# Where the tiles of a decoder trunk's matmuls lie in SBUF: tile widths rounded up to 64 bytes, and pads between pools

## The chip, the cores and the metric

The kernel runs on one core of a Trainium2 chip. The metric is the device time of one execution in microseconds; lower is better. The engines are called as in the profile: PE is TensorE's matmul and PEld its weight load, DVE is VectorE, ACT is ScalarE, POOL is GpSimd and SP is SyncE. A PE matmul has two operands in SBUF: the stationary one (the weights, 128 columns, loaded by a weight load of its own before the matmul) and the moving one (256 or 512 columns, streamed through the array).

## What is computed

A trunk of two decoder layers on 512 tokens of width 1024, in float32. The first layer mixes tokens by a gated delta rule, the second by windowed attention with sinks; both also attend to 256 fixed memory tokens, and both end in a SwiGLU feed-forward of width 2816.

```python
def swiglu(h, w_gate_up, w_down):
    gu = h @ w_gate_up
    return (jax.nn.silu(gu[..., :D_FF]) * gu[..., D_FF:]) @ w_down

for layer in range(DEPTH):                        # 2
    h = rms_norm(x, ln_mix[layer])
    mkv = mem_n @ w_mem_kv[layer]
    if layer < N_A_LAYERS:
        mix_out, mem_q = gated_deltanet_mixer(h, gdn_w_in[a], ...)
    else:
        proj = h @ swa_w_q[bl]
        mix_out = sliding_window_attention(q, shared_k, shared_v, swa_sinks[bl])
    mem_o = memory_attention(mem_q, mem_k, mem_v)
    x = x + jnp.concatenate([mix_out, mem_o], axis=-1) @ w_out[layer]
    x = x + swiglu(rms_norm(x, ln_ffn[layer]), w_gate_up[layer], w_down[layer])
    ...
return rms_norm(x, ln_final)
```

## The kernel before

**Matmuls in three parts.** Every large product keeps float32 accuracy by splitting each operand into a high and a low part (`split`, L166: a rounding copy on ACT writes the high part, a subtraction on DVE the low part). `mm3` (L191) then issues three matmuls for one tile of 128 x 128 weights: high weights by high activations, high weights by low activations, low weights by high activations. They run in the format float32r, four bytes an element. 2,436 of them have 512 moving columns and 3,672 have 256; together they are most of what PE does.

**Where the operands live.** SBUF is given out by pools that lie one behind the other in each partition. From the left: `const` (constants, gains, small vectors), `w` (raw weights and a ring of three pairs of split weights, `whi` and `wlo`), `acta` and `actb` (eight pairs of split activations each, `h` and `l`; layer 0 and layer 1 use the two in turn for the input of the feed-forward and for its first eight activations), `x` (the residual stream). From the right, one after the other in time: `early` and `gdn` of the first layer, `ffn0`, `swa`, `ffn1`. A feed-forward pool holds, among others, the split sums of tokens (`T`, the tiles of `token_sums`, eight), the activations beyond the eighth (`ac8` to `ac11`), and work tiles (`fg`, `fu`, `fs`, `ws`).

**The feed-forward.** For a pair of columns `quarters` makes seven products of 256 columns from eight quarter blocks in place of eight, out of sums of weights (`wraw`, `ws`) and sums of tokens (`T`); three of the seven use `h` tiles directly, four use `T`. Each product is four `mm3`, so 12 matmuls in a row. The first four gate columns are plain products of 512 columns. The way down (`wdn`) is again made of `mm3` with 512 columns over the activations `h`, then `ac8`, `ac9` and so on.

**Order.** The program is written in the order of the source, and a scheduler places independent instructions on each engine's queue by priority and by which buffers are free. Within one engine the queue runs in order.

**Small tiles that the change touches.** `scores` (L710) makes three vectors of eight numbers (`mx`, `den`, `nm`) for each block of heads, and `weigh` (L748) a fourth, `es`. `token_sums` makes `minus` (four negated gains) once a layer and `fc` (128 x 256) four times a layer, in one buffer. `eps` holds two constants.

Of the kernel before, what the change touches and what calls it, by code (L numbers as in the profile page):

```python
# [9 lines left out]
F32 = mybir.dt.float32  # L10
# [5 lines left out]
PSUM = bass.MemoryType.PSUM  # L16
DRAM = bass.MemoryType.DRAM

P = 128
T = 512  # L20
D = 1024
KD = D // P
H = 6
NC = 4
# [2 lines left out]
DFF = 2816  # L27
FT = DFF // P
EPS = 1e-6
NEG = -1e30  # L30
BASE = 32
NB = P // BASE
# [34 lines left out]
def constants():  # L67
# [4 lines left out]
    c[:, C_ONE:C_ONE + P] = 1.0  # L72
    c[:, C_CAUS:C_CAUS + P] = np.where(i[None, :] >= i[:, None], 0.0, NEG)
    c[:, C_BAND:C_BAND + P] = np.where(i[None, :] > i[:, None], 0.0, NEG)
# [12 lines left out]
class Builder:  # L87
# [6 lines left out]
    def t(self, pool, shape, dtype=F32, tag=None, bufs=None, name=None):  # L94
        self.n += 1
        nm = f"{name or tag}_{self.n}"
        kw = {}
        if tag is not None:
            kw["tag"] = tag
        if bufs is not None:  # L100
            kw["bufs"] = bufs
        return pool.tile(shape, dtype, name=nm, **kw)

    @contextmanager
    def banks(self, **bufs):
# [121 lines left out]
    def build(self):  # L227
        tc, nc, a = self.tc, self.nc, self.a
        with ExitStack() as st:
            opened = lambda name, **kw: tc.tile_pool(name=name, bufs=1, reuse_waits="tile", **kw)  # L230
            pool = lambda name, **kw: st.enter_context(opened(name, **kw))
            cp = pool("const")
            self.wpool, self.apool = pool("w"), pool("acta")
            self.dpool = pool("scratch", space=DRAM)
            self.load_constants(cp)
            self.weng = nc.vector
            with opened("layer0", side="right") as self.mpool:
                with self.banks(pj=3, g=2, sc=3):
                    with opened("early", side="right") as ep:
                        self.mem_and_norm(ep)  # L240
                        self.gates(ep)
                    with opened("gdn", side="right") as gp:
                        mix = self.gdn(gp)
                    self.bpool, xp = pool("actb"), pool("x")
                    self.x = [self.t(xp, [P, T], F32, f"x{k}") for k in range(KD)]
                    for k in range(KD):
                        nc.sync.dma_start(self.x[k], a["xT"][:, k, :])
                    self.rstd, self.cosT, self.sinT = (self.t(xp, [P, T], F32, n) for n in ("rstd", "cosT", "sinT"))
                    h = self.output(xp, 0, mix, self.bpool)
            with opened("ffn0", side="right") as fp, self.banks(pj=2, g=6):  # L250
                self.ffn(fp, xp, 0, h, self.apool, rope=True)
            with self.banks(pj=2, g=1, qk=1, pt=2, sc=1):
                with opened("swa", side="right") as sp:
                    mix = self.swa(sp)
                h = self.output(xp, 1, mix, self.apool)
            with opened("ffn1", side="right") as fp, self.banks(pj=2, g=6):
                self.ffn(fp, xp, 1, h, self.bpool)

    def load_constants(self, cp):
        nc, a = self.nc, self.a  # L260
        c = self.t(cp, [P, C_N], F32, "consts")
        g = self.t(cp, [P, G_N], F32, "gains")
        s = self.t(cp, [P, 24], F32, "small")
        nc.sync.dma_start(g, a["gains"])
        self.consts, self.gains, self.small = c, g, s
        self.ident = c[:, C_ID:C_ID + P]
        self.U = c[:, C_U:C_U + P]
        self.ones = c[:, C_ONE:C_ONE + P]
        self.caus = c[:, C_CAUS:C_CAUS + P]
        self.band = c[:, C_BAND:C_BAND + 2 * P]  # L270
        self.one = c[:, C_ONE:C_ONE + 1]
        v = self.t(cp, [P, 2], F32, "eps")
        nc.vector.memset(v[:, 0:1], EPS)
        nc.vector.memset(v[:, 1:2], EPS * EPS * P)
        self.eps, self.epsq = v[:, 0:1], v[:, 1:2]
# [178 lines left out]
    def gdn(self, gp):  # L454
# [89 lines left out]
        for h0 in (0, 3):  # L544
# [3 lines left out]
            for h, t in zip(range(h0, h0 + 3), ts):  # L548
# [6 lines left out]
                sq = self.t(gp, [P, T], F32, "sq", 1)  # L555
                nc.scalar.activation(sq, t, AF.Square, scale=math.sqrt(EPS) * P)
                q2.append(self.t(self.dpool, [P, T], F32, f"q2{h}"))
# [152 lines left out]
    def scores(self, pool, q, kk, win):  # L710

        nc = self.nc
        own = "pt" in self.pbufs
        half = [slice(0, 64), slice(64, P)]
        sm = [self.t(pool, [P, 2, 2, 2 * P], F32, "sm", 4 if own else 2) for _ in range(2)]
        sm = [t[:, n] for t in sm for n in range(2)]
        mx = self.t(pool, [P, 2 * NC], F32, "mx", 2)
        den = self.t(pool, [P, 2 * NC], F32, "den", 2)
        nm = self.t(pool, [P, 2 * NC], F32, "nm", 2)
        for n0 in range(0, NC, 2):  # L720
            if own:
                two = self.bank("qk", [P, 2, 2, 2 * P])
                ps = [two[:, b] for b in range(2)]
            else:
                ps = [self.bank("sc" if n0 else "g", [P, 2, 2 * P]) for _ in range(2)]
            for n in (n0, n0 + 1):
                ks = slice((n - 1) * P if n else 0, (n + 1) * P) if win else slice(0, ML)
                c0 = P if win and n == 0 else 0
                for b in range(2):
                    self.scored = self.mm(ps[b][:, n - n0, c0:], q[half[b], n * P:(n + 1) * P], kk[half[b], ks])  # L730
            for b in range(2):
                i = b * NC + n0
                if win:
                    for n in (n0, n0 + 1):
                        c0 = 0 if n else P
                        nc.vector.tensor_tensor_reduce(  # L736
                            out=sm[n][:, b, c0:], in0=ps[b][:, n - n0, c0:], in1=self.band[:, c0:], scale=1.0,
                            scalar=NEG, op0=ALU.add, op1=ALU.max, accum_out=mx[:, b * NC + n:b * NC + n + 1])
                else:
                    nc.vector.tensor_reduce(out=mx[:, i:i + 2], in_=ps[b], op=ALU.max, axis=AX.X)  # L740
                    self.ts(nm[:, i:i + 2], mx[:, i:i + 2], -0.125, ALU.mult)
                    for n in (n0, n0 + 1):
                        i = b * NC + n
                        self.fn(sm[n][:, b, :], ps[b][:, n - n0, :], AF.Exp, scale=0.125, bias=nm[:, i:i + 1],
                                accum_out=den[:, i:i + 1])
        return sm, mx, den, nm

    def weigh(self, pool, scores, vv, m, out, sinks):  # L748

# [1 line left out]
        win = sinks is not None  # L751
        own = "pt" in self.pbufs
        half = [slice(0, 64), slice(64, P)]
        sm, mx, den, nm = scores
        if win:
            sk = sinks.unsqueeze(2).to_broadcast([P, 2, NC])
            v4 = lambda ap: ap.rearrange("p (b n) -> p b n", b=2)
            self.stt(v4(mx), v4(mx), 0.125, sk, ALU.mult, ALU.max)
            self.ts(nm, mx, -1.0, ALU.mult)
            es = self.t(pool, [P, 2 * NC], F32, "es", 2)  # L760
            self.tt(nc.vector, v4(es), v4(nm), sk, ALU.add)
            self.fn(es, es, AF.Exp)
            for n in range(NC):
                c0 = 0 if n else P
                for b in range(2):
                    i = b * NC + n
                    self.fn(sm[n][:, b, c0:], sm[n][:, b, c0:], AF.Exp, scale=0.125, bias=nm[:, i:i + 1],
                            accum_out=den[:, i:i + 1])
            self.tt(nc.vector, den, den, es, ALU.add)
# [3 lines left out]
        for n in range(NC):  # L773
# [3 lines left out]
            p = sm[n][:, :, k0 * P:]  # L777
# [21 lines left out]
            for n, t in pf.items():  # L799
                for j in range(1 if win and n == 0 else 0, 2):  # L800
                    for b in range(2):
                        v = vv[n - 1 + j][:, half[b]] if win else vv[j][:, m * P + 64 * b:m * P + 64 * b + 64]
# [23 lines left out]
    def ffn(self, fp, xp, layer, h, apool, rope=False):  # L826
# [3 lines left out]
        acts, sums, open_pairs, places = [], [], [], []  # L830
# [12 lines left out]

        def put(u):
            n = len(acts)
            acts.append(self.pair(apool) if n < KD else self.pair(fp, f"ac{n}"))
            self.split(u, *acts[-1])

        def ring():
# [30 lines left out]
        for f0, half in ((0, 12), (12, 10)):  # L880
# [16 lines left out]
            for m in range(tail):  # L897
                ps = self.bank("pj")
                for j in (0, 6):
                    n = min(6, half - j)  # L900
# [8 lines left out]
        if tail < KD:  # L909
# [9 lines left out]
            for t in parts:  # L919
                acc = self.acc[:, t]  # L920
                for m in range(tail, KD):
# [3 lines left out]
                    x = self.x[m][:, t]  # L925
# [11 lines left out]
    def token_sums(self, fp, layer, j, h):  # L937


        q = T // 2  # L940
        if j == 0:
            self.minus = self.t(fp, [P, 4], F32, "minus")
            self.ts(self.minus, self.gains[:, G_FFN[layer] + 4:G_FFN[layer] + 8], -1.0, ALU.mult)
        g0, g1 = (self.gain(G_FFN[layer], j + i) for i in (0, 4))
        n1 = self.minus[:, j:j + 1]
        x0, x1 = self.x[j], self.x[j + 4]
        c = self.t(fp, [P, q], F32, "fc")
        raw = [self.t(fp, [P, T], F32, "ws", 4) for _ in range(2)]
        t = [x[:, i * q:(i + 1) * q] for x in raw for i in range(2)]
        self.ts(c, x0[:, q:], g0, ALU.mult)  # L950
# [272 lines left out]
```

## Time and profile before

| | |
|---|---|
| median of 3 runs | 1167.77 us (1166.97 to 1170.53) |
| the profiled execution | 1172.62 us, of which the span from the first to the last instruction is 1170.9 us |
| granted TensorE clock | 0.995 of full speed, mean over the span |
| PE busy | 1144.3 us, 98% of the span, 7,476 matmul records |
| PEld busy | 1001.0 us, 85% |
| DVE, ACT, POOL busy | 844.7 us (72%), 636.6 us (54%), 85.8 us (7%) |
| DMA engines | 131 GB/s on average over the span |

A row of the timeline gives the start of an instruction from the span's start, its duration, engine, source line, operation, the tiles as output<-inputs (for a matmul the moving operand first), and the shape; two neighbours with the same names are merged as x2. Buffer numbers are left out of names, so `h` stands for any of the eight. A matmul's duration is longer than its distance to the next matmul, since matmuls overlap; it is the distance between two starts that adds up to the time.

### The profile page before, as it was taken

How to read it: one execution, taken by the hardware profiler on the slowest of the kernel's cores; microseconds unless marked ns; L12 is line 12 of the kernel's file. 1: busy time of each engine (PE TensorE's matmuls, PEld its weight loads, DVE VectorE, ACT ScalarE, POOL GpSimd, SP SyncE). 2: the span in 40 equal slices, each digit the busy share in tenths (PEclk: the TensorE clock that was granted, in tenths of full speed). 3: DMA queues.
4: the chain of work that ended last, by engine and by line, in shares of the span. 5: the costliest groups of instructions: out<-in, count | busy, mean ns of one | idle time of the engine just before them, and what ended most of it. 6: DMA issues, size and time to landing. Idle time of an engine off the chain costs nothing.

```text
span 1170.9 us, 19669 instructions
## 1 busy us (share of the span) xinstructions
PE 1144.3 (98%) x7476; PEld 1001.0 (85%) x7476; DVE 844.7 (72%) x1587; ACT 636.6 (54%) x1273; POOL 85.8 (7%) x97
## 2 busy tenths in 40 slices
PE   7999999999989999999999999999999999999996
PEld 6878777877889998899998777678899988999986
DVE  5754977767769987479876767859699843798754
ACT  7569573366546652246654536675566622466533
POOL 0210000000021100111100000000211100111000
PEclk9999999999989999999999999999999999999999
DMA  8333352225377744557723421113777743577232
GB/s 305 126 109 115 112 126 92 74 89 162 118 176 175 182 127 124 154 147 184 180 74 98 131 90 38 36 50 115 183 185 183 176 111 101 150 187 178 73 91 95
DMA packets 73971, 152.83 MB, mean 131 GB/s; under 512 B 17756, under 2 KB 18420, under 8 KB 73876
## 3 DMA queue, kind: packets, MB, share of 16 engines
q1 hardware_dynamic: 62356, 130.59, 36.0%
q0 software_dynamic: 11520, 20.98, 11.3%
q8 instruction: 59, 0.97, 0.3%
q14 instruction: 36, 0.29, 0.1%
HBM read 144.58 MB, written 6.96 MB: 129 GB/s over the span
## 4 chain that ended last, share of the span: by engine, by line
PE 65%; DVE 3%; ACT 1%; issue 0%; DVEq 0%; ACTq 0%
PE g L144 35%; PE pj L144 28%; PE pt L148 1%; PE sc L144 1%; ACT sm L132 1%; DVE wlo L151 1%; DVE sm L736 0%; DVE l L154 0%; PE qk L144 0%; DVE q L151 0%; DVE rs L1059 0%; DVE rs L151 0%; DVE sm L158 0%; DVE fu L151 0%; DVE l L151 0%
## 5 line engine op out<-in xcount | busy, mean ns | idle before, releaser
L138 ACT ACTIVATE whi<-wraw 128x512 fp32r<-128x512 f32 (+2 forms) x331 | 245.0, 747 | 271.4 <-PE pj L144 177.7
L151 DVE TENSOR_TENSOR wlo<-wraw,whi 128x512 fp32r<-128x512 f32 (+2 forms) x331 | 274.8, 839 | 106.0 <-ACT whi L138 100.3
L144 PE MATMUL pj<-h,whi 128*128 128x512 f32 (+1 forms) x676 | 266.0, 395 | 0.2
L144 PE MATMUL pj<-l,whi 128*128 128x512 f32 (+1 forms) x676 | 264.9, 392 | 0.3 <-DVE l L154 0.3
L144 PE MATMUL pj<-h,wlo 128*128 128x512 f32 (+1 forms) x676 | 265.0, 392 | 0.0
L144 PE MATMUL g<-T,whi 128*128 128x256 f32 x1280 | 233.4, 283 | 3.0 <-ACT fs L138 3.0
L144 PEld LDWEIGHTS g<-T,whi 128*128 128x128 f32 x1280 | 197.7, 190 | 4.8 <-ACT fs L138 3.2
L144 PE MATMUL g<-T,wlo 128*128 128x256 f32 x640 | 180.8, 282 | 0.0
L144 PEld LDWEIGHTS pj<-h,whi 128*128 128x128 f32 x676 | 126.9, 188 | 29.3 <-issue 3.1
L144 PEld LDWEIGHTS pj<-l,whi 128*128 128x128 f32 x676 | 127.0, 188 | 27.5 <-issue 2.0
L144 PEld LDWEIGHTS pj<-h,wlo 128*128 128x128 f32 x676 | 127.2, 188 | 26.6 <-issue 1.9
L144 PE MATMUL g<-h,wlo 128*128 128x256 f32 (+1 forms) x508 | 147.2, 290 | 0.0
L144 PE MATMUL g<-h,whi 128*128 128x256 f32 (+1 forms) x508 | 147.0, 289 | 0.0
L144 PE MATMUL g<-l,whi 128*128 128x256 f32 (+1 forms) x508 | 146.8, 289 | 0.0
L144 PEld LDWEIGHTS g<-T,wlo 128*128 128x128 f32 x640 | 121.0, 189 | 0.2 <-DVE wlo L151 0.2
L144 PEld LDWEIGHTS g<-h,whi 128*128 128x128 f32 x508 | 97.3, 192 | 1.2
L144 PEld LDWEIGHTS g<-l,whi 128*128 128x128 f32 x508 | 97.2, 191 | 1.2
L144 PEld LDWEIGHTS g<-h,wlo 128*128 128x128 f32 x508 | 97.2, 191 | 1.2 <-issue 0.2
L972 POOL DMA_DIRECT2D ws<-in_wgu x40 | 35.1, 879 | 747.9 <-DMA ws<-in_wgu 541.1
L138 ACT ACTIVATE whi<-ws 128x512 fp32r<-128x512 f32 x80 | 50.5, 632 | 58.5 <-PE g L144 43.1
L151 DVE TENSOR_TENSOR fu<-pj,rstd 128x512 f32<-128x512 f32 (+1 forms) x34 | 22.4, 660 | 56.5 <-PE pj L144 56.5
L151 DVE TENSOR_TENSOR wlo<-ws,whi 128x512 fp32r<-128x512 f32 x80 | 54.9, 686 | 7.3 <-ACT whi L138 7.2
(345 smaller groups left out, 1634.0 us busy)
## 6 DMA issues: line engine op xcount, KB each, us to landing
wraw<-in_wgu SPq DMA_DIRECT2D x48, 512.0 KB, 4.3
ws<-in_wgu SPq DMA_DIRECT2D x80, 256.0 KB, 3.6
ws<-in_wgu POOLq DMA_DIRECT2D x80, 256.0 KB, 4.8
wraw<-in_wdn SPq DMA_DIRECT2D x48, 384.0 KB, 3.1
wraw<-in_win SPq DMA_DIRECT2D x26, 512.0 KB, 3.7
wraw<-in_wgu SPq DMA_DIRECT2D x40, 256.0 KB, 4.4
wraw<-in_wout SPq DMA_DIRECT2D x16, 512.0 KB, 3.6
wraw<-in_wdn SPq DMA_DIRECT2D x16, 256.0 KB, 2.6
```

What stands on the lines that cost most here:

```text
L132: ins = self.nc.scalar.activation(out, in_, func, **kw).ins
L138: self.copied = self.nc.scalar.activation(out, in_, AF.Copy, **kw).ins
L144: return self.nc.tensor.matmul(out, lhsT, rhs, start=start, stop=stop, skip_group_check=more).ins
L148: return self.nc.tensor.transpose(out, in_, self.ident[:k, :k]).ins
L151: return eng.tensor_tensor(out=out, in0=a, in1=b, op=op).ins
L972: nc.gpsimd.dma_start(s1, a22, accum_op=ALU.add)
```

## The change

It changes where tiles lie. The helper that makes a tile rounds its width up to a multiple of 64 bytes. Empty tiles (`room`) are put at the front of `acta`, `actb` and `x`, ahead of `ac8` in each feed-forward pool and behind `ac11`; an empty tile of 32 bytes (`edge`) is put at the right end. To make place, `mx`, `den`, `nm` and `es` become one tile `stats`, `minus` of both layers moves into the tile `eps`, and `fc` takes a buffer of the work tile `fs`, which has three.

```diff
+LINE = 64
+ROOM = {"acta": 64, "actb": 128, "x": 64, "acts": (64, 64), "end": (224, 96)}
...
+        width = LINE // mybir.dt.size(dtype)
+        n = math.prod(shape[1:])
+        if pool.space not in (PSUM, DRAM) and n % width:
+            flat = pool.tile([shape[0], -(-n // width) * width], dtype, name=nm, **kw)[:, :n]
...
         return pool.tile(shape, dtype, name=nm, **kw)
+    def room(self, pool, size):
+        if size:
+            self.n += 1
+            pool.tile([P, size // 4], F32, name=f"room_{self.n}")
...
+            self.room(self.apool, ROOM["acta"])
...
+            pool("edge", side="right").tile([P, 8], F32, name="edge")
...
+                    self.room(self.bpool, ROOM["actb"])
+                    self.room(xp, ROOM["x"])
...
-        v = self.t(cp, [P, 2], F32, "eps")
+        v = self.t(cp, [P, 10], F32, "eps")
+        self.minuses = [v[:, 2 + 4 * i:6 + 4 * i] for i in range(2)]
...
-        mx = self.t(pool, [P, 2 * NC], F32, "mx", 2)
-        den = self.t(pool, [P, 2 * NC], F32, "den", 2)
-        nm = self.t(pool, [P, 2 * NC], F32, "nm", 2)
+        stats = self.t(pool, [P, 4, 2 * NC], F32, "stats", 2)
+        mx, den, nm, es = (stats[:, i, :] for i in range(4))
...
+            if n == KD and not f0:
+                self.room(fp, ROOM["acts"][layer])
             acts.append(self.pair(apool) if n < KD else self.pair(fp, f"ac{n}"))
+            if n == 11 and not f0:
+                self.room(fp, ROOM["end"][layer])
...
-            self.minus = self.t(fp, [P, 4], F32, "minus")
+            self.minus = self.minuses[layer]
...
-        c = self.t(fp, [P, q], F32, "fc")
+        c = self.t(fp, [P, q], F32, "fs", 3)
```

The addresses in the two built programs show what this does to the split matmuls. The table gives the start of the operand within 256 bytes, the distance (moving less stationary, modulo 256) and the number of matmuls. The weights' ring lies at 96 before and at 192 now; every later block of 128 weights in it starts a multiple of 512 bytes further.

| moving tiles | columns | matmuls | start before | start now | distance before | distance now |
|---|---|---|---|---|---|---|
| `acta` | 512 | 1,440 | 96 | 0 | 0 | 64 |
| `actb` | 512 | 672 | 96 | 128 | 0 | 192 |
| `acta` | 256 | 720 | 96 | 0 | 0 | 64 |
| `actb` | 256 | 768 | 96 | 128 | 0 | 192 |
| `T` of layer 0 | 256 | 960 | 224 | 160 | 128 | 224 |
| `T` of layer 1 | 256 | 960 | 224 | 32 | 128 | 96 |
| `ac8` to `ac11`, layer 0 | 512 | 144 | 224 | 224 | 128 | 32 |
| `ac8` to `ac11`, layer 1 | 512 | 132 | 224 | 96 | 128 | 160 |
| memory tokens and weights, early | 256 | 192 | 224 or 96 | 192 | 128 | 0 |
| `mq0`, `mq1` | 512 | 48 | 224 | 192 | 128 | 0 |
| last block of layer 1 | 256 | 72 | several | several | 128 or 0 | 96, 64 or 160 |

Before, all of them start 32 bytes behind a multiple of 64. Now the weights' ring, `acta`, `actb`, the memory tokens and `mq` start on a multiple of 64; `T` and the `ac` tiles still start 32 bytes behind one.

PE's queue is the same instruction for instruction, and so is POOL's. On DVE a few small instructions move. At the program's start, the queue of DVE before (`ml` is the low part of the memory tokens, `mh` the high part):

```order
L273 MEMSET eps_70 128x1
L274 MEMSET eps_70 128x1
L154 SCALAR_TENSOR_TENSOR ml_85<-mem_82,gains_67,mh_84 128x256 x2
L151 TENSOR_TENSOR wlo_137<-wraw_87,whi_136 128x512
L154 SCALAR_TENSOR_TENSOR ml_85<-mem_82,gains_67,mh_84 128x256 x2
```

And with the change:

```order
L293 MEMSET eps_71 128x1
L294 MEMSET eps_71 128x1
L173 TENSOR_SCALAR eps_71<-gains_68 128x4 x2
L169 SCALAR_TENSOR_TENSOR ml_90<-mem_87,gains_68,mh_89 128x256 x2
L166 TENSOR_TENSOR wlo_142<-wraw_92,whi_141 128x512
```

The two negations of gains that stood at the head of each feed-forward now stand ahead of the first split of the memory tokens. At the start of layer 0's feed-forward, where DVE makes the sums of tokens (`ws` are raw sums, `T` their low parts, `sqa` the running sum of squares), its queue before:

```order
L151 TENSOR_TENSOR sqa_3036<-sqa_2996,sq_3034 128x512
L158 TENSOR_SCALAR minus_3125<-gains_67 128x4
L158 TENSOR_SCALAR fc_3127<-x_538_2741,gains_67 128x256
L154 SCALAR_TENSOR_TENSOR ws_3128<-x_538_2741,gains_67,fc_3127 128x256
L154 SCALAR_TENSOR_TENSOR ws_3129<-x_542_2745,gains_67,fc_3127 128x256
L154 SCALAR_TENSOR_TENSOR ws_3128<-x_542_2745,minus_3125,ws_3128 128x256
L158 TENSOR_SCALAR fc_3175<-x_539_2742,gains_67 128x256
```

And with the change:

```order
L166 TENSOR_TENSOR sqa_3039<-sqa_2999,sq_3037 128x512
L173 TENSOR_SCALAR fs_3129<-x_537_2744,gains_68 128x256
L173 TENSOR_SCALAR fs_3177<-x_538_2745,gains_68 128x256
L169 SCALAR_TENSOR_TENSOR ws_3130<-x_537_2744,gains_68,fs_3129 128x256
L169 SCALAR_TENSOR_TENSOR ws_3131<-x_541_2748,gains_68,fs_3129 128x256
L169 SCALAR_TENSOR_TENSOR ws_3130<-x_541_2748,eps_71,ws_3130 128x256
L169 SCALAR_TENSOR_TENSOR ws_3178<-x_538_2745,gains_68,fs_3177 128x256
```

The negation is gone from here, and the first step of the second sum stands ahead of the work on the first, since it no longer shares one buffer with it. The same holds for the third and fourth sums and for layer 1; ACT, which writes the high parts of the sums, follows with a few exchanges of neighbours, and SP exchanges two loads of weights once.

More of the change, by code (lines that the diff above doesn't have):

```diff
@@ L101, in t @@
             kw["bufs"] = bufs
+        width = LINE // mybir.dt.size(dtype)
+        n = math.prod(shape[1:])
+        if pool.space not in (PSUM, DRAM) and n % width:
+            flat = pool.tile([shape[0], -(-n // width) * width], dtype, name=nm, **kw)[:, :n]
+            if len(shape) == 2:
+                return flat
+            names = "abcdef"[:len(shape) - 1]
+            return flat.rearrange(f"p ({' '.join(names)}) -> p {' '.join(names)}", **dict(zip(names, shape[1:])))
         return pool.tile(shape, dtype, name=nm, **kw)
+    def room(self, pool, size):
+        if size:
+            self.n += 1
+            pool.tile([P, size // 4], F32, name=f"room_{self.n}")
     @contextmanager
@@ L745, in scores @@
                                 accum_out=den[:, i:i + 1])
-        return sm, mx, den, nm
+        return sm, mx, den, nm, es
     def weigh(self, pool, scores, vv, m, out, sinks):
@@ L753, in weigh @@
         half = [slice(0, 64), slice(64, P)]
-        sm, mx, den, nm = scores
+        sm, mx, den, nm, es = scores
         if win:
@@ L759, in weigh @@
             self.ts(nm, mx, -1.0, ALU.mult)
-            es = self.t(pool, [P, 2 * NC], F32, "es", 2)
             self.tt(nc.vector, v4(es), v4(nm), sk, ALU.add)
```

## The prediction

> **What bounds the kernel now.** The page says first who is busy, then whose work the chain that ended last is made of.
>
> ```profile
> span 1170.9 us, 19669 instructions
> PE 1144.3 (98%) x7476; PEld 1001.0 (85%) x7476; DVE 844.7 (72%) x1587; ACT 636.6 (54%) x1273; POOL 85.8 (7%) x97
> PE 65%; DVE 3%; ACT 1%; issue 0%; DVEq 0%; ACTq 0%
> ```
>
> PE is without work for 2% of the span only, so nothing that other engines wait for can be worth much; the time is the number of matmuls by the distance at which they start. The chain in order of time has its longest pieces in the feed-forwards, and the busy times by stretch say how much cover there is in one of them (the columns are the stretch, its length, then PE, PEld, DVE, ACT and POOL busy with their counts, PE's clock, DMA share and GB/s).
>
> ```profile
> 341.80 98.48 PE g L144 x804
> 443.07 64.86 PE pj L144 x283
> 507.93 98.45 PE g L144 x828
> ```
>
> ```profile
> 507.00:608.00 101.00, 101.00 (x842) 100.33 (x842) 87.45 (x156) 62.70 (x118) 12.94 (x15) 1.00 0.63 155
> ```
>
> In this stretch, the second half of layer 0's feed-forward, PE never stops, at full clock, while DVE has 13.6 us of 101 to spare: the products can start up to 13% closer together before DVE becomes the bound. So the question is what sets the distance of two matmuls. The timeline shows it where nothing else interferes. First 512 columns over `acta` and `actb` tiles (operands at distance 0 before), 120 steps between these two rows; then 512 columns over `ac` tiles (distance 128), 12 steps:
>
> ```profile
> 788.26 0.39 PE L144 MATMUL pj<-h,whi 128*128 128x512 f32 x1
> ...
> 815.46 0.39 PE L144 MATMUL pj<-h,whi 128*128 128x512 f32 x1
> ```
>
> ```profile
> 447.25 0.40 PE L144 MATMUL pj<-ac8h,whi 128*128 128x512 f32 x1
> ...
> 450.04 0.39 PE L144 MATMUL pj<-h,whi 128*128 128x512 f32 x1
> ```
>
> 27.20 us over 120 is 226.7 ns; 2.79 us over 12 is 232.5 ns. Then 256 columns over `h` (distance 0), 15 steps, and over `T` (distance 128), 36 steps:
>
> ```profile
> 523.10 0.28 PE L144 MATMUL g<-h,whi 128*128 128x256 f32 x1
> ...
> 524.90 0.40 PE L144 MATMUL g<-T,whi 128*128 128x256 f32 x2
> ...
> 527.75 0.40 PE L144 MATMUL g<-T,whi 128*128 128x256 f32 x2
> ...
> 532.02 0.28 PE L144 MATMUL g<-h,whi 128*128 128x256 f32 x1
> ```
>
> That is 120.0 ns and 118.6 ns. The groups by form tell how much of the program this is:
>
> ```profile
> L144 PE MATMUL pj<-h,whi 128*128 128x512 f32 x660 | 261.5, 397 | 0.2
> ...
> L144 PE MATMUL g<-T,whi 128*128 128x256 f32 x1280 | 233.4, 283 | 3.0 <-ACT fs L138 3.0
> ...
> L144 PE MATMUL g<-h,wlo 128*128 128x256 f32 x480 | 136.1, 283 | 0.0
> ...
> L144 PE MATMUL pj<-ac8h,whi 128*128 128x512 f32 x30 | 11.8, 395 | 0.0
> ...
> L144 PE MATMUL pj<-ac8l,whi 128*128 128x512 f32 x30 | 11.6, 387 | 0.0
> ```
>
> **What the distances say.** 226.7 less 120.0 is 106.7 ns for 256 more columns: 0.417 ns a column, so 16 columns, which are 64 bytes, take 6.67 ns. In this unit the four distances are 34.0 and 34.9 for 512 columns, 18.0 and 17.8 for 256. The columns themselves need 32 and 16 units. So at distance 0 a matmul costs exactly two units more than its columns, whatever its length; at distance 128 it costs 2.9 or 1.8. That the cost comes in whole units of 64 bytes, and that it changes with the place of the operands alone (same engine, same clock, same weights' ring), is what I build on.
>
> [...]
>
> **The change, part by part.** First the aligned operands. Before, every split operand starts 32 bytes behind a multiple of 64, so 512 columns (2,048 bytes) touch 33 pieces of 64 bytes and 256 columns touch 17, one more than needed; a weight block of 512 bytes touches 9 and not 8. If operands are fetched in such pieces, one of the two extra units is this piece. With the change 2,160 matmuls of 512 columns (`acta` 1,440, `actb` 672, `mq` 48) and 1,680 of 256 (720, 768, early 192) have both operands on a multiple of 64. One unit less for each is 14.4 + 11.2 = 25.6 us. No row of before shows an aligned pair of this format, so this is bounded: below by both extra units, twice as much; above by the 5.8 ns that 512 columns lose at distance 128, where a clash of the two reads instead of the piece would be what costs. I take the one unit, since at distance 0 the cost is a whole number of units for both lengths.
>
> Some of these matmuls do not stand on the chain: at the start and in the second layer's attention, PE waits for other engines.
>
> ```profile
> 0.00:100.00 100.00, 91.63 (x500) 75.66 (x501) 58.87 (x93) 70.52 (x169) 13.96 (x15) 1.00 0.49 169
> ...
> 667.00:780.00 113.00, 109.85 (x720) 82.39 (x718) 78.50 (x244) 70.41 (x208) 0.00 (x0) 1.00 0.18 57
> ```
>
> PE is idle for 8.4 and 3.2 us there, 11.5 of 213; an estimate from this is that 6% of the gain is lost, which leaves 24 us.
>
> Second, the operands that stay 32 bytes behind a multiple of 64 but change their distance: 1,920 matmuls on `T` (from 128 to 224 and 96), 276 on `ac` tiles (to 32 and 160), 72 at the end. Their weights are aligned now, they are not. Rows for such distances do not exist; the two known ones give 118.6 and 120.0 ns for 256 columns, so from -1 unit (the weights' piece, 1,920 by 6.67 = 12.8 us less) to +1.4 ns (2.7 us more); for `ac` from -6 to +5 ns, under 2 us either way. I take 0 for both.
>
> Third, the small tiles. `minus` moves to the front of DVE's queue, and DVE sits waiting there for ACT's first high part anyhow:
>
> ```profile
> L158 DVE TENSOR_SCALAR minus<-gains x2: 158/160/161, 310.9 to 780.9; 128x4 f32<-128x4 f32 x2
> ```
>
> ```profile
> 6.05 0.88 DVE L154 SCALAR_TENSOR_TENSOR ml<-mem,gains,mh 128x256 fp32r<-128x256 f32 x2 [5.15 <-ACT mh L138]
> ```
>
> Two by 0.16 us lie in an idle time of 5.15 us, if the gains have landed by then, as ACT's first high part needs them too; without that cover it is 0.3 us. The first steps of the token sums run earlier on DVE, while PE works on plain gate products; the only PE wait near them is the 3.0 us before a `T` product in the group above, whose releaser is ACT's copy `fs`, so between 3.0 us gained and as much lost, and I take 0. `stats` in place of four tiles leaves the instructions of the attention in their order. Padding costs no time, only place.
>
> Sum: 24 us less. The profiled execution took 1172.6 us (span 1170.9), 0.4% above the median of the runs; 1172.6 - 24 = 1148.6, and from the median 1167.8 - 24 = **1143.8 us**.
>
> What could take the gain away is the next bound: at 113.3 ns in place of 120.0 for `h`, the stretch of 101 us shrinks by 360 matmuls by 6.67 ns = 2.4 us, and DVE's 87.5 us still fit.
>
> **The rivals.**
>
> The slower one: distance 0 is not a bad place but a good one. There the two reads fall into step and stay there, as 120 equal steps show; at distance 128 they do not, and the durations of neighbours differ (395 and 387 ns above). If only distance 0 falls into step, the new distances behave like 128: 2,112 matmuls of 512 columns go from 226.7 to 232.5 (+12.3 us), 1,488 of 256 from 120.0 to 118.6 (-2.1 us): 1178.0 us, and 1180.7 if `T` loses its 1.4 ns as well. For it: the one other distance that the trace has is worse for 512 columns. Against it: 256 columns are better there, and alignment plays no part in it. It decides as soon as 512 columns over `acta` stand more than 226.7 + 0.7 = 227.4 ns apart, where the 0.7 ns is what 2.1 us are on 2,112 matmuls and more with every one that 256 columns fail to gain.
>
> No difference: the two extra units belong to something that does not depend on addresses, the change-over of weights for instance, and 128 is an odd case of its own. Then it is 1167.8. For it: the cost is the same for both lengths, as a cost per matmul would be.
>
> A larger gain: both extra units were clashes and go. That is 51.2 us on 3,840 matmuls, 48 on the chain, 1119.8 us. For it: nothing in the rows but that columns alone would need 213.3 and 106.7 ns. [...]
>
> That the change does not do what it says is ruled out by the addresses in the program.
>
> **How the numbers follow.** A measurement of this kernel tells 0.3%, 3.5 us, from no change. One unit gained: 0.45. The slower rival: 0.38, since the only known step away from distance 0 costs time where 512 columns are concerned. No difference: 0.10. The larger gain: 0.07. So faster 0.52, same 0.10, slower 0.38. The forecast's own range is 1131 (`T` gains a unit, too) to 1155 (half the unit lost); since cases of both signs hold most of the chance, the whole range reaches from 1128, a little below that, to 1181, the upper end of the slower rival. It leaves out the larger gain and the tails.
>
> **What would show it.** In the timeline of the changed kernel, a run of `pj<-h` matmuls of 512 columns stands 220.0 ns apart if the forecast is right, 226.7 if nothing changed, 230 or more in the slower rival; `g<-h` with 256 columns 113.3, 120.0 or below 120. `T` products stay at about 118.6. Stretches in which only PE works shorten in proportion, and the share of idle PE time stays at 2%. The forecast is wrong if `pj<-h` keeps 34 units or more on aligned tiles: then the 64-byte pieces are not what the second unit is made of.

## The result and the profile after

The changed kernel takes 1172.91 us (median of 4 runs, 1172.13 to 1173.37) against 1167.37 us before: a ratio of 1.0038, with a 95% interval of 1.0022 to 1.0053. It is 5.5 us slower; a gain of 24 us was forecast.

The page of the changed kernel, traced in a run of 1172.13 us, looks as before: span, busy times and shares of the chain that ended last.

```profile
span 1170.3 us, 19669 instructions
PE 1145.7 (98%) x7476; PEld 997.2 (85%) x7476; DVE 843.9 (72%) x1587; ACT 636.8 (54%) x1273; POOL 85.9 (7%) x97
PE 65%; DVE 3%; ACT 1%; issue 0%; DVEq 0%; ACTq 0%
```

PE is still the bound, busy for 98% of the span at a granted clock of 0.997 in the mean. What changed is the distance of its starts. First the timeline of the changed kernel for 512 columns: 110 steps over `acta` (distance 64 now), then 140 over `actb` (192 now).

```profile
104.73 0.40 PE L159 MATMUL sc<-h,whi 128*128 128x512 f32 x1
...
129.91 0.40 PE L159 MATMUL pj<-h,wlo 128*128 128x512 f32 x1
...
779.52 0.39 PE L159 MATMUL g<-h,whi 128*128 128x512 f32 x1
...
812.18 0.39 PE L159 MATMUL pj<-h,wlo 128*128 128x512 f32 x1
```

And the same two stretches before, both at distance 0:

```profile
105.26 0.40 PE L144 MATMUL sc<-h,whi 128*128 128x512 f32 x1
...
130.24 0.39 PE L144 MATMUL pj<-h,wlo 128*128 128x512 f32 x1
...
783.46 0.40 PE L144 MATMUL g<-h,whi 128*128 128x512 f32 x1
...
815.24 0.39 PE L144 MATMUL pj<-h,wlo 128*128 128x512 f32 x1
```

25.18 us over 110 is 228.9 ns, where it was 24.98 over 110, 227.1 ns; 32.66 over 140 is 233.3 ns, where it was 31.78 over 140, 227.0 ns. Neither is near the 220.0 forecast. With 256 columns, in the changed kernel: 23 steps over `h` (distance 192), then 35 over `T` in layer 0 (224) and in layer 1 (96).

```profile
342.29 0.28 PE L159 MATMUL g<-h,whi 128*128 128x256 f32 x1
...
345.00 0.28 PE L159 MATMUL g<-h,wlo 128*128 128x256 f32 x1
...
347.95 0.40 PE L159 MATMUL g<-T,whi 128*128 128x256 f32 x2
...
352.09 0.28 PE L159 MATMUL g<-T,wlo 128*128 128x256 f32 x1
...
845.24 0.40 PE L159 MATMUL g<-T,whi 128*128 128x256 f32 x2
...
849.43 0.28 PE L159 MATMUL g<-T,wlo 128*128 128x256 f32 x1
```

These are 117.8, 118.3 and 119.7 ns (starts are printed to 0.01 us, which leaves 0.3 ns open over 35 steps); before it was 120.0 at distance 0 and 118.6 at 128. The following table gives the mean step over the whole trace, worked out from the starts of all split matmuls (a step that holds a wait is left out), and what it makes of the time.

| tiles, columns | matmuls | step before, ns | step now, ns | us |
|---|---|---|---|---|
| `acta`, 512 | 1,440 | 227.7 | 229.3 | +2.3 |
| `actb`, 512 | 672 | 227.7 | 233.4 | +3.8 |
| `acta` and `actb`, 256 | 1,488 | 119.1 | 117.7 | -2.2 |
| `T` of layer 0, 256 | 960 | 118.75 | 118.3 | -0.4 |
| `T` of layer 1, 256 | 960 | 118.75 | 120.0 | +1.2 |
| `ac`, memory and `mq` | 516 | | | +0.4 |

Together +5.1 us, of which not all can reach the end, since some of these matmuls stand where PE waits for others anyhow. The experiments show a second cost, from the new order of small instructions; the traces put it at one wait.

### The profile page after: what moved, and what is told of

Same layout as the page of the kernel before. It is cut to its first block, busy times and chain, and to the rows that moved or that the text cites. A ratio compares the mean times of both kernels' runs of the same rounds, so it can differ in the third digit from the quotient of the medians.

```text
span 1170.3 us, 19669 instructions
## 1 busy us (share of the span) xinstructions
PE 1145.7 (98%) x7476; PEld 997.2 (85%) x7476; DVE 843.9 (72%) x1587; ACT 636.8 (54%) x1273; POOL 85.9 (7%) x97
## 4 chain that ended last, share of the span: by engine, by line
PE 65%; DVE 3%; ACT 1%; issue 0%; DVEq 0%; ACTq 0%
PE g L159 35%; PE pj L159 28%; PE pt L163 1%; PE sc L159 1%; ACT sm L147 1%; DVE wlo L166 1%; DVE sm L755 0%; DVE l L169 0%; PE qk L159 0%; DVE q L166 0%; DVE rs L1081 0%; DVE rs L166 0%; DVE sm L173 0%; DVE fu L166 0%; DVE l L166 0%
```

## The experiments

In all of them PE's queue is that of before, instruction for instruction. The diffs are against the changed kernel, where nothing else is said. "Order of before" stands for two edits in `token_sums` that give DVE, ACT and SP back the order they had, while the places stay free to choose:

```diff
-            self.minus = self.minuses[layer]
+            self.minus = self.t(fp, [P, 4], F32, "minus")
-        c = self.t(fp, [P, q], F32, "fs", 3)
+        if j == 0:
+            self.c = self.t(fp, [P, q], F32, "fs", 3)
+        c = self.c
```

### Alignment or distance

All operands aligned, all at distance 0:

```diff
-ROOM = {"acta": 64, "actb": 128, "x": 64, "acts": (64, 64), "end": (224, 96)}
+ROOM = {"acta": 0, "actb": 0, "x": 0, "acts": (0, 0), "end": (0, 0)}
```

> The changed kernel with its pads taken out: weights, activations, T and the ac tiles all start at 192 modulo 256, so every operand stays on a multiple of 64 bytes and every distance is 0. The queues of all engines are those of the changed kernel. Theory D (the distance alone counts, alignment is worth nothing): pj<-h with 512 columns goes back to 226.7 ns, 256 columns lock at 120.0 ns, T too; time 1167 to 1170 us, as before. Rival A (a 64-byte piece is saved on aligned operands as forecast, and distances 64 and 192 lost more than that): 220.0 and 113.3 ns, some 40 us less than before, 1127 to 1145 us. Rival S (places do nothing, the exchanged small instructions on DVE and ACT cost the 5.5 us): 1173 us.

Measured: 1172.65 us, 1.0032 (1.0019 to 1.0045). The time agrees with rival S, the steps with theory D. Its timeline, 140 steps over `actb` and 35 over `T`, all aligned:

```profile
782.49 0.39 PE L159 MATMUL g<-h,whi 128*128 128x512 f32 x1
...
814.29 0.39 PE L159 MATMUL pj<-h,wlo 128*128 128x512 f32 x1
...
349.99 0.40 PE L159 MATMUL g<-T,whi 128*128 128x256 f32 x2
...
354.19 0.28 PE L159 MATMUL g<-T,wlo 128*128 128x256 f32 x1
```

227.1 and 120.0 ns: on multiples of 64 bytes, distance 0 costs what it cost 32 bytes behind them. Rival A is out. Some 2 of the 4.6 us by which this run is slower lie in its steps: over the whole trace `T`, now at 0, takes 1.2 ns more on 1,920 matmuls (+2.3 us), `h` between `T` products 0.9 ns more on 1,488 (+1.3), and `ac`, now at 0, 5.7 ns less on 276 (-1.6). The rest asks for a second cause.

The distances of before, with the changed code:

```diff
+            self.room(cp, 32)
-            pool("edge", side="right").tile([P, 8], F32, name="edge")
+ROOM = {"acta": 0, "actb": 0, "x": 0, "acts": (0, 0), "end": (128, 128)}
```

> The changed kernel's instructions, in its order, with weights and activations at 224 modulo 256 (distance 0) and T and the ac tiles at 96 (distance 128): the distances of before, none on a multiple of 64. Theory D: 1167 us, pj<-h at 226.7 ns, g<-T at 118.7 ns. Rival A: the same, 1167 us. Rival S: 1173 us, since the merged small tiles and the exchanged instructions are all in it.

Measured: 1171.18 us, 1.0020 (1.0009 to 1.0031), between what theory D and rival S said. The steps are those of before to 0.1 ns (227.7, 119.2, `T` 118.8), so these 2 to 3 us are not in the steps.

The new distances, 32 bytes on:

```diff
+            self.room(cp, 32)
-            pool("edge", side="right").tile([P, 8], F32, name="edge")
```

> The changed kernel with everything moved 32 bytes on: the distances stay 64 and 192 for the activations, 224 and 96 for T, but now weights and activations start 32 bytes behind a multiple of 64 and T starts on one. Theory D: as the changed kernel, 1173 us, pj<-h steps of 226, 229, 232 in turn over acta and 231, 236 over actb. Rival A: 3,840 matmuls lose a piece of 6.67 ns each (+25.6 us) and 1,920 on T gain one (-12.8 us): 1186 us.

Measured: 1174.84 us, 1.0046 (1.0031 to 1.0061), not the 1186 us of rival A. Step for step it is the changed kernel: 229.4 over `acta`, 233.4 over `actb`, 117.8 and 117.6 on `h`, 118.3 and 120.0 on `T`.

One place moved in the kernel before, and nothing else:

```diff
             self.wpool, self.apool = pool("w"), pool("acta")
+            self.t(self.apool, [P, 24], F32, "room")
```

> The kernel before with a pad of 96 bytes in front of acta, so that acta and actb go from distance 0 to 96; T and ac stay at 128 and all queues stay as they are. Theory D: 2,112 matmuls of 512 columns go from 227.7 to 233.4 ns (+12.0 us), 1,488 of 256 from 119.1 to 119.9 (+1.1 us), of which waits for other engines take up about a third as in the run with the other distances: 1176 to 1181 us. Rival (distance matters little, the changed kernel's loss is its new order): under 1170 us.

Measured: 1177.47 us, 1.0073 (1.0053 to 1.0093). Its 140 steps over `actb`:

```profile
783.90 0.40 PE L144 MATMUL g<-h,whi 128*128 128x512 f32 x1
...
816.57 0.39 PE L144 MATMUL pj<-h,wlo 128*128 128x512 f32 x1
```

233.4 ns against 227.0. Here the activations moved by 96 bytes and the weights stayed, and the steps changed; in the run above all operands moved by 32 bytes together, and they did not. So what counts is where the moving operand lies against the stationary one, at 6.4 ns a matmul here; the run does not show where inside a step the time goes.

The distances that were left:

```diff
+ROOM = {"acta": 96, "actb": 128, "x": 64, "acts": (64, 64), "end": (192, 64)}
-            pool("edge", side="right").tile([P, 8], F32, name="edge")
```

> The distances not tried yet: acta at 96, actb at 224, T at 32 in layer 0 and at 160 in layer 1, ac tiles at 96 and 224. Theory D: every distance has a step of its own that repeats; the five known ones for 512 columns lie at 226.7 (0), 229.0 (64) and 232 to 234 (the others), those for 256 between 117.6 and 120.0, so 512 columns here 229 to 234 ns and 1169 to 1180 us. Rival 0 (only distance 0 and multiples of 64 are good): odd multiples of 32 all at 232 to 234 ns for 512 columns, 1177 to 1181 us.

Measured: 1176.07 us, 1.0061 (1.0039 to 1.0083). 512 columns take 233.4 ns at 96 and 233.3 at 224, 256 columns 119.8 at 96, 118.2 at 224, 118.0 at 160, and 116.9 at 32. With these the table of distances is whole: 512 columns have their one good place at 0 (227.5), a middling one at 64 (229.4), and 232.4 to 233.9 everywhere else.

### The second cost: one wait, and the clock behind it

The kernel before again, for a second trace:

> The kernel before, unchanged, for a second trace. Its runs lie at 1167 to 1168 us or at 1169.5 to 1172.5; the traced one took 1172.6 and has a wait of 3.3 us before the fourth weight block's T product at the start of layer 0's feed-forward, with the following 30 matmuls at half clock (213 ns for 256 columns). Theory W (that wait is what differs between its runs): a run near 1167.5 has a wait under 2 us there and no matmul at half clock; a run near 1171 shows both. Rival: the difference lies elsewhere.

Measured: 1167.82 us in a single run, as theory W had it. The wait is at the start of layer 0's feed-forward, before the third of the first pair's seven products (the expectation calls it the fourth block's), and its chain begins with a transfer. The rows of the timelines show: POOL issues the transfer that adds the second part of the pair's first weight sum `ws`; POOL issues the same one of the next pair; ACT's split of `ws` starts when the first has landed; PE starts the third product. The first trace of before (1172.6 us):

```profile
328.73 1.01 POOL L972 DMA_DIRECT2D ws<-in_wgu  x1 [264.86 <-DMA ws<-in_wgu]
...
332.46 0.86 POOL L972 DMA_DIRECT2D ws<-in_wgu  x1 [1.81 <-DMA ws<-in_wgu]
...
335.38 0.63 ACT L138 ACTIVATE whi<-ws 128x512 fp32r<-128x512 f32 x1 [6.53 <-DMA ws<-in_wgu]
...
341.80 0.80 PE L144 MATMUL g<-T,whi 128*128 128x256 f32 x2 [3.03 <-ACT fs L138]
```

The second one:

```profile
328.16 1.01 POOL L972 DMA_DIRECT2D ws<-in_wgu  x1 [264.92 <-DMA ws<-in_wgu]
...
332.33 0.87 POOL L972 DMA_DIRECT2D ws<-in_wgu  x1 [2.25 <-DMA ws<-in_wgu]
...
333.13 0.63 ACT L138 ACTIVATE whi<-ws 128x512 fp32r<-128x512 f32 x1 [4.64 <-DMA ws<-in_wgu]
...
339.56 0.50 PE L144 MATMUL g<-T,whi 128*128 128x256 f32 x2 [1.41 <-ACT fs L138]
```

From issue to split the transfer takes 6.65 us in one run and 4.97 in the other; PE idles 3.03 or 1.41 us. From the split to PE it is 6.4 us in both, along DVE's and ACT's queues. Then the 6 us behind the wait, in both (columns as in the prediction, the clock is the third from the end):

```profile
341.80:347.80 6.00, 6.00 (x28) 6.00 (x29) 2.84 (x6) 2.27 (x5) 1.40 (x2) 0.50 0.90 244
```

```profile
339.50:345.50 6.00, 5.95 (x50) 5.95 (x51) 4.89 (x9) 3.14 (x8) 1.91 (x3) 1.00 0.91 254
```

After the long wait PE runs at half clock and does 28 matmuls in the time of 50. Up to the wait the two traces differ by 0.6 us, behind the slow matmuls by 4.9, and by no more until the end. So these two runs differ by this wait and the clock behind it; that it accounts for the spread of all runs of a kernel is not shown, since other traces have half clock elsewhere, too, as told below.

One line of the change in the kernel before:

```diff
-        c = self.t(fp, [P, q], F32, "fc")
+        c = self.t(fp, [P, q], F32, "fs", 3)
```

> The kernel before with one line of the change: token_sums takes fc from the three buffers of fs. No operand of a split matmul moves modulo 256; the orders on DVE and ACT are those of the changed kernel there. Theory O (this order makes the wait at the start of layer 0's feed-forward longer and brings the half clock in nearly all runs): 1170.5 to 1171.5 us, like the run with the old distances. Rival (rounding of tiles and the other merges cost it): 1167.5 us.

Measured: 1170.94 us, 1.0020 (1.0009 to 1.0032), the same as the changed code at the old distances: this line is the second cost. Its trace (of a run of 1174.9 us), and the changed kernel's:

```profile
330.70 1.01 POOL L972 DMA_DIRECT2D ws<-in_wgu  x1 [266.44 <-DMA ws<-in_wgu]
...
333.27 0.87 POOL L972 DMA_DIRECT2D ws<-in_wgu  x1 [0.66 <-DMA ws<-in_wgu]
...
337.61 0.63 ACT L138 ACTIVATE whi<-ws 128x512 fp32r<-128x512 f32 x1 [7.63 <-DMA ws<-in_wgu]
...
344.11 0.79 PE L144 MATMUL g<-T,whi 128*128 128x256 f32 x2 [3.02 <-ACT fs L138]
```

```profile
328.88 1.01 POOL L994 DMA_DIRECT2D ws<-in_wgu  x1 [265.67 <-DMA ws<-in_wgu]
...
331.23 0.86 POOL L994 DMA_DIRECT2D ws<-in_wgu  x1 [0.43 <-issue]
...
334.27 0.64 ACT L153 ACTIVATE whi<-ws 128x512 fp32r<-128x512 f32 x1 [6.17 <-DMA ws<-in_wgu]
...
340.77 0.50 PE L159 MATMUL g<-T,whi 128*128 128x256 f32 x2 [1.64 <-ACT fs L153]
```

In the new order the sums give their `ws` buffers back in other steps, and the next pair's transfer is issued 2.6 or 2.35 us behind the first, where it was 3.7 and 4.2; the first then takes 6.9 and 5.4 us. The order is shown to be the cause. That the two transfers slow each other is read from the traces and was not tried apart: in the ten traces in which the second is issued 4.1 us or more behind the first, the first takes 4.9 to 5.3 us from issue to split, and in the eight with 3.8 us or less (all six with the new order) 5.3 to 6.9. In the six traces with the new order the distance of the two starts at this wait is 1.7, 1.9, 2.7, 2.9, 3.3 and 3.3 us, and in the last four half clock follows, for 15 to 21 matmuls some 213 ns apart; of the twelve with the old order it follows in two, at 3.3 us, while the other ten have 0.9 to 1.9 us and none. So at this wait a distance of 2.7 us was enough and one of 1.9 us was not. That is no general bound: at a wait near 139 us, half clock followed a distance of 2.5 us in the run with `T` at 32 (clock 0.50 from 140.1 to 143.4 us) and none followed 2.4 us in the run with `T` at 32 and 288 (clock 1.00); and in the trace of the one changed line the clock is 0.50 from 198.9 to 202.2 us, behind a stretch of small matmuls (32 x 32 and 64 x 64) in which PE was busy throughout.

The changed places with the order of before:

> The changed kernel with all its places, but the sums of tokens share one buffer again and minus is made where it was, so that DVE, ACT and SP have the order of the kernel before. Theory D+O (distances and order are two separate costs): the distances alone, which were 3.1 us from the start of layer 0's feed-forward on in the changed kernel's trace against the second trace of before, remain: about 1171 us, a wait under 2 us before the fourth weight block's T product in layer 0, no half clock in most runs. Rival (the order costs nothing when the distances are new): 1173 us. Rival (the distances cost nothing): 1167.5 us.

Measured: 1171.39 us, 1.0022 (1.0013 to 1.0031), with 1.1 us at the wait and full clock behind it. Distances alone cost 0.22%, the order alone 0.20%, both together 0.38%: two separate costs.

### Two steps at one distance

`T` at 32, the best distance of the table for 256 columns, in the kernel before:

```diff
             acts.append(self.pair(apool) if n < KD else self.pair(fp, f"ac{n}"))
+            if n == 11 and not f0:
+                self.t(fp, [P, 24], F32, "room")
```

> The kernel before with one pad of 96 bytes behind ac11 in each feed-forward pool, nothing else: T and the ac tiles go from distance 128 to 32, all queues stay as they are. Theory D: 1,920 products on T go from 118.75 to 116.9 ns (-3.5 us), 276 on ac stay at 232.5: 1164 us. Rival (the steps of 256 columns are the same work by another name, and the time is set elsewhere): 1167.5 us.

Measured: 1168.24 us, 0.9994 (0.9984 to 1.0004), no difference. `T` took 118.0 ns and not 116.9, and its neighbours on `h` rose to 119.7. A distance does not fix the step by itself.

Order of before, `T` at 32 and 288:

```diff
+ROOM = {"acta": 0, "actb": 0, "x": 0, "acts": (224, 224), "end": (256, 0)}
```

> Order of before, weights and activations at 192 modulo 256 (distance 0), ac tiles at distance 0 modulo 256, T at 32 modulo 512 in layer 0 and at 288 modulo 512 in layer 1, both 32 modulo 256. Distance 32 gave 116.9 ns in one run (288 modulo 512) and 118.0 in another (32 modulo 512). Theory M (the distance modulo 512 counts there): T at 118.0 ns in layer 0 and 116.9 in layer 1. Theory H (what was streamed before, or the place of the weights, counts): the same step in both layers. Either way the ac tiles gain 5 ns on 276 matmuls (-1.3 us) and T 0.8 to 1.9 ns on 1,920 (-1.4 to -3.5 us); h may lose 0.9 ns on 1,488 (+1.3 us) as in the run with T at 32: 1164 to 1167 us.

Measured: 1164.92 us, 0.9969 (0.9957 to 0.9980). `T` took 118.0 in both layers, so theory M fell, and H stands so far: with `T` starting at 224 and the weights at 192, modulo 256, it is 116.6 ns between products on `h` at 224 (first pair of rows, from the run with the other distances), and 118.0 between products on `h` at 0 (second pair, the 32 modulo 512).

```profile
348.75 0.40 PE L159 MATMUL g<-T,whi 128*128 128x256 f32 x2
...
352.83 0.28 PE L159 MATMUL g<-T,wlo 128*128 128x256 f32 x1
```

```profile
346.96 0.40 PE L159 MATMUL g<-T,whi 128*128 128x256 f32 x2
...
351.09 0.28 PE L159 MATMUL g<-T,wlo 128*128 128x256 f32 x1
```

The two runs that followed, again with the order of before, have `T` at 64 and 192 with `h` at 0, and `T` at 32 with `h` at 192 and 64:

```diff
+ROOM = {"acta": 0, "actb": 0, "x": 0, "acts": (192, 64), "end": (0, 0)}      # the first
+ROOM = {"acta": 64, "actb": 128, "x": 64, "acts": (64, 64), "end": (160, 160)}   # the second
```

> Order of before, weights, activations and ac tiles at distance 0, T at 64 in layer 0 and 192 in layer 1. Theory D (each distance has its step, as measured on h: 117.8 at 64 and 117.6 at 192, against 118.0 for T at 32 in the run that mixed 32 and 288): another 0.3 ns on 1,920 products, 1164.3 us, 3 us under the kernel before. Theory H (the step of T depends on what its neighbours leave behind, as between 116.9 and 118.0 at distance 32): T between 117 and 120 ns, 1162.5 to 1168 us.

> The changed places with the order of before, but T at distance 32 in both layers; its neighbours on h have distance 192 in layer 0 and 64 in layer 1. T at 32 took 116.9 ns between products on h at 224, and 118.0 between products on h at 0, with T and the weights at the same places. Theory H (neighbours decide): T takes another step than 118.0 in at least one layer. Rival (118.0 is the step of 32, and the 116.9 belongs to something else of that run): 118.0 in both.

Measured: 1162.02 us, 0.9941 (0.9925 to 0.9958), and 1163.2 us in a single run. In the first, `T` in layer 0 (64) and in layer 1 (192):

```profile
348.64 0.40 PE L159 MATMUL g<-T,whi 128*128 128x256 f32 x2
...
352.77 0.28 PE L159 MATMUL g<-T,wlo 128*128 128x256 f32 x1
...
843.80 0.40 PE L159 MATMUL g<-T,whi 128*128 128x256 f32 x2
...
847.78 0.28 PE L159 MATMUL g<-T,wlo 128*128 128x256 f32 x1
```

118.0 and 113.7 ns; once settled, the second repeats 113, 113, 114: 113.3, exactly the one unit (6.67 ns) below 120 that was forecast. Neither theory had named a step this low. In the second run `h` takes 114.0 at 64 and 114.4 at 192, where the changed places with the order of before took 117.8 and 117.6; of the neighbours of `h` in these products only `T` differs. `T` at 32 took 117.0. Both runs speak for what is at the core of H, that the neighbours change the step at one distance.

Four runs, with the order of before, asked whether the unit belongs to alignment after all, and what picks the step:

```diff
+ROOM = {"acta": 0, "actb": 0, "x": 0, "acts": (64, 64), "end": (0, 0)}       # T at 192, h at 0
+ROOM = {"acta": 64, "actb": 0, "x": 0, "acts": (64, 64), "end": (0, 0)}      # T at 192, h at 64
+ROOM = {"acta": 64, "actb": 0, "x": 0, "acts": (192, 192), "end": (0, 0)}    # T and h at 64
+self.room(cp, 32), no edge, and the first of these                         # T at 192, h at 0, all 32 bytes on
```

> Order of before, weights, activations and ac tiles at 192 modulo 256 (distance 0), T at distance 192 in both layers. Theory L (two locked steps exist at distances 64 and 192, 117.7 and 113.3 ns, and the step that a product finds is set by its neighbours): T behind h at distance 0 took 113.3 at 192 and 118 at 64, so 114 ns in both layers, 3.6 us less than with 64 in layer 0: 1158 to 1159 us. Rival (the 113.3 belongs to layer 1's tiles): 118 ns in layer 0 and 1162 us.

> As the run before in this list, but acta and actb at distance 64. Theory L: 2,112 matmuls of 512 columns lose 2 ns (+4.2 us); h with 256 columns goes to 113.3 ns if its neighbours leave it there (1,488 by 6.2 ns, -9.2 us), to 117.8 if not (-2.5 us); T at 113.3 or 117.7 likewise (0 or +7 us). So 1153 if both lock low, 1167 if neither.

> acta, actb and T at distance 64, ac tiles at 0. Theory L: h and T share one distance, so nothing disturbs the lock between products, and all 256-column matmuls take the same step: 1153 us if it is 113.3 ns, 1167 us if it is 117.8. Rival (each product finds its own step by its own operands): a mixture.

> The kernel with T at distance 192 in both layers, with everything moved 32 bytes on: no operand of a split matmul starts on a multiple of 64. Rival A (the 6.67 ns that 113.3 is below 120 are the 64-byte piece of the forecast, saved by aligned operands): T at 120 ns or above, 1170 us. Theory L (the relation of the two operands alone): T at 114 ns in both layers, the same time as the aligned one.

Measured: 1156.97 us, 0.9908 (0.9891 to 0.9925), for `T` at 192 and `h` at 0, the fastest of all: 114.0 ns over these 35 steps, 114.2 in the mean of each layer.

```profile
346.42 0.40 PE L159 MATMUL g<-T,whi 128*128 128x256 f32 x2
...
350.41 0.28 PE L159 MATMUL g<-T,wlo 128*128 128x256 f32 x1
```

With everything 32 bytes on, no operand of a split matmul aligned: 1157.14 us, 0.9907 (0.9890 to 0.9924), and 113.7 ns over the same 35 steps (113.9 in both runs before rounding).

```profile
347.47 0.40 PE L159 MATMUL g<-T,whi 128*128 128x256 f32 x2
...
351.45 0.28 PE L159 MATMUL g<-T,wlo 128*128 128x256 f32 x1
```

So the unit is real, and alignment is not what it is made of. `h` and `T` both at 64 or 192, where the starts lock on one of two steps (113.3 or 117.7 ns, repeated from matmul to matmul), gave 1163.73 (0.9971, 0.9953 to 0.9989; runs from 1161.7 to 1171.0) and 1163.11 us (0.9966, 0.9950 to 0.9981; runs from 1159.4 to 1167.7). Both lie between the 1153 us that theory L gave for the low step everywhere and its 1167 for the high one. The trace of the last shows what can spread them. Its `T` products in layer 1, at the same distance, in the first and in the second half of the feed-forward:

```profile
842.80 0.39 PE L159 MATMUL g<-T,whi 128*128 128x256 f32 x2
...
846.77 0.28 PE L159 MATMUL g<-T,wlo 128*128 128x256 f32 x1
...
1034.62 0.40 PE L159 MATMUL g<-T,whi 128*128 128x256 f32 x2
...
1038.74 0.28 PE L159 MATMUL g<-T,wlo 128*128 128x256 f32 x1
```

113.4 and 117.7 ns over 35 steps each. Both steps are stable at one distance: all of layer 1's first half ran at the low one, `h` and `T` alike, and after the way down in between all of the second half at the high one. Where `h` lies at 0, its matmuls, 0.12 us apart, stand between the `T` products, and `T` at 192 then settles on 113.3 within four matmuls, each time (114.2 in the mean of each layer of the fastest run); `T` at 64 settles on 117.7 (118.0 over the 35 steps above).

## Why the prediction was wrong

**The unit of 64 bytes, from the rows: wrong in its reading.** The step was "If operands are fetched in such pieces, one of the two extra units is this piece", on which the whole 25.6 us hung. Aligned operands at distance 0 keep 227.1 and 120.0 ns, and the 6.67 ns appear without any alignment (113.9 ns over 35 steps with everything 32 bytes on). That the cost at distance 0 comes in whole units of 64 bytes did not say what it is made of, and elsewhere settled steps are no whole units: 117.8 ns is 17.7 of them, 116.7 ns 17.5. I took the whole number for a number of pieces fetched. What the extra time is made of instead stays open; shown is that it goes by the distance of the two operands and by the neighbouring products.

**The slower rival: right in sign and in its core, too large.** Distance 0 is the good place for 512 columns (227.7 ns in the mean, 229.3 and more elsewhere). That two reads fall into step there was my reading of the equal steps; no run looked inside a step. But 64 is not like 128: 1,440 matmuls lost 1.6 ns and not 5.8. `actb` at 192 lost the full 5.7, and 256 columns gained the 1.4 ns that the rival gave them. With these sizes its +12.3 - 2.1 us become +6.1 - 2.2, from the first three lines of the table.

**`T` and `ac`: inside their bounds.** -0.4 and +1.2 us where 0 was taken between -12.8 and +2.7; under 0.5 us for the rest.

**The small tiles: mis-sized, inside their bounds.** "I take 0", between 3.0 us gained and as much lost, and the wait that it named is the one that decided. It costs 0.20%, 2.3 us. I read the releaser, ACT's copy `fs`, and not the chain behind it, which starts 13 us earlier with POOL's transfer; so the exchanged steps on DVE seemed to have no one waiting. Half clock behind it, which the prediction did not reckon with, made the longer waits dearer (28 matmuls in the time of 50). `minus` at the front of DVE cost nothing that shows: the first split matmul starts at 7.16 us, 7.11 in the second trace of before.

**The cover: right.** PE is still 98% busy and DVE 72%, and no other engine became the bound. Some two of the 5.1 us in the steps did not reach the end: against the second trace of before, the changed kernel is 0.4 us later at the start of the first feed-forward, 1.1 us later behind the wait, and 4.2 us later at its last split matmul, so that 3.1 us came from the steps behind the wait.

**The other rivals.** "No difference" is out by the interval, the larger gain by the steps.

## What to carry to other kernels

Where PE is the bound, measure the distance between starts by where the two operands lie against each other, for each length apart, before reckoning a gain from any rule about alignment; here 96 bytes in front of one pool cost 0.73%, and the layout with `T` at 192 and the rest at 0, with the order kept, gave 0.92%. A step can have two stable values at one layout (113.4 and 117.7 ns in one trace here), so the product before it belongs to the layout as well, and a layout that takes the same value each time can be worth more than one that can take either of two: here its runs took 1156.6 to 1159.2 us, and those of the two with `h` and `T` at 64 or 192 took 1159.4 to 1171.0. Follow a wait on a bound engine back past its releaser to the transfer it began with (13 us earlier here), and look for half clock right behind it (28 matmuls in 6 us here, 50 without it).

## What had not been expected of the hardware

Mean steps of split matmuls repeat to about 0.1 ns between runs at the same distances (at those of before 227.7 and 227.7 ns, 119.1 and 119.2, 118.75 and 118.8; at the new ones 229.3 and 229.4, 233.4 and 233.4), except where `h` and `T` both lie at 64 or 192, and depend on the distance of the two operands modulo 256 bytes (`T` at 384 took the 118.8 ns that it took at 128, and at 288 the 118.0 that it took at 32): 227.5 ns for 512 columns at 0, 229.4 at 64, 232.4 to 233.9 at the other six; with 256 columns the order is another, from 120.0 at 0 and at 96 down to 113.3 at 64 and 192. At these two the steps 113.3 and 117.7 are both stable. What picks one of them when `h` lies at one of these two as well, and why `T` behind `h` at 0 found the low one at 192 (114.0 and 113.7 ns over 35 steps) and the high one at 64 (118.0), stays open; no run looked at what the reads do within one step.
